# Modulation steps during the first layer's projections: from VectorE to GpSimd and ScalarE

## The chip, the cores and the metric

The kernel is one program on one core of a Trainium2 chip. The metric is the device time of one execution in microseconds (us); the median of three runs before the change is 1866.89 us. TensorE is called PE, VectorE DVE, ScalarE ACT, GpSimd POOL, and the queue that issues the DMAs SP.

## The reference

Two layers of a diffusion backbone, for 512 latent tokens and 256 context tokens of width 1024. The part that is changed is the modulation: two condition vectors, `c` for the latent tokens and `c_ctx` for the context tokens, each times a matrix of 1024 x 6144 per layer.

```python
def modulation(cond, w, b):
    m = jax.nn.silu(cond) @ w + b
    m = m.reshape(cond.shape[:-1] + (6, D_MODEL))
    return [m[..., i, None, :] for i in range(6)]

for l in range(DEPTH):
    mx = modulation(c, ada_w[l], ada_b[l])
    mc = modulation(c_ctx, ada_w[l], ada_b[l])
    hx = rmsnorm(x, norm_pre_mix[l]) * (1.0 + mx[1]) + mx[0]
    px = hx @ w_in[l]
    ...
    x = x + mx[2] * rmsnorm(yx, norm_post_mix[l])
    hx = rmsnorm(x, norm_pre_mlp[l]) * (1.0 + mx[4]) + mx[3]
    x = x + mx[5] * rmsnorm(sq_relu_mlp(hx, mlp_w1[l], mlp_w2[l]), norm_post_mlp[l])
```

Between these lines stand four token mixers (a gated delta net, a short convolution, a Hyena long convolution and a neighbourhood attention), fed by `px` and the same projection `pc` of the context.

## The kernel before

All large products are matmuls in three parts: `load_w` loads a weight tile of 128 x 512 (`raw`, three buffers), ACT casts it (`whi`, line 126), DVE subtracts to get the rest (`wlo`, line 127), and `mm3` (lines 138 to 140) makes three matmuls of each pair of halves. `big` (line 145 on) makes one output block of 128 columns with them: four `whi`/`wlo` pairs are held at a time, the result goes to `mx` (two PSUM buffers, latent tokens) and `mc` (one PSUM buffer, context tokens), and `dwconv` reads it out with a scaled copy on ACT (line 382) and two steps on DVE (lines 383 and 385).

The first two of the six modulation rows of layer 0 are made by matmuls at the start. The other ten row groups come from a generator, `mod_steps` (line 248). Each of its 80 steps loads a block of 128 x 1024 of the transposed matrix (`adrow`, two buffers, line 254) and makes, for each half of 512 and each condition, one multiplication with the broadcast condition `cbc` whose row sum goes to `part` (line 258). On DVE that is a SCALAR_TENSOR_TENSOR and the readout of its accumulator. A step of the stretch that matters has two halves and two conditions, so four such pairs. Every eighth step two small additions make the finished rows `mod`.

The steps are asked for at fixed places by `step_mods`: three after each of the four projections of keys and queries (`gdn_project`, line 561 on, `GPM = 3`), so 12 steps and 48 pairs, and the rest later, beside the mixers and the MLP. That is only the place in the program's text. A scheduler sets the order of each engine from the data that an instruction needs and its own costs; within one engine the order is then fixed. A step needs nothing but its block of weights, so the scheduler can place it early: in the trace the 12 steps run from 82 to 202 us, beside the projections and, more than half of them, beside the Hyena branch that comes ahead of these: `hyena_project` (three pairs of projections, with `spectrum` between them, whose sums and differences `ha` POOL makes at lines 472 and 473), and `hyena`, where ACT copies `odd` (line 510) out of PSUM before a long row of products on DVE. After that come the projections of keys and queries, `gdn_normalise` (DVE with two steps on POOL, lines 731 and 733), and the triangular solve of the delta net.

Of the kernel before, what the change touches and what calls it, by code (L numbers as in the profile page):

```python
# [9 lines left out]
F32 = mybir.dt.float32  # L10
F32R = mybir.dt.float32r
BF16 = mybir.dt.bfloat16
AF = mybir.ActivationFunctionType
# [32 lines left out]
class Net:  # L46
# [193 lines left out]
    def cond_rows(self, p):  # L240

        self.cbc = p.tile([128, 2, D], F32, tag="cbc", name="cbc")
        self.junk = p.tile([128, 512], BF16, tag="junk", name="junk")
        self.ring(p, "ad", 2)
        self.nc.sync.dma_start(self.cbc, self.cdr[0].partition_broadcast(128))

    def mod_steps(self):

        nc = self.nc
        for l, i in [(0, i) for i in range(2, 6)] + [(1, i) for i in range(6)]:  # L250
            conds = (0,) if l == 1 and i > 1 else (0, 1)
            for nb in range(i * 8, i * 8 + 8):
                raw = self.row_block()
                nc.sync.dma_start(raw, self.a["adaD"][32 + nb if l else nb - 16])
                for h in range(2):
                    hs = slice(h * 512, (h + 1) * 512)
                    for cnd in conds:
                        nc.vector.scalar_tensor_tensor(self.junk, raw[:, hs], 1.0, self.cbc[:, cnd, hs], op0=OP.mult,  # L258
                                                       op1=OP.mult, accum_out=self.part[:, l, cnd, nb, h:h + 1])
                if nb % 8 == 7:  # L260
                    s = slice(i * 8, i * 8 + 8)
                    for cnd in conds:
                        m = self.mod[:, l, cnd, s]
                        nc.vector.tensor_add(m, self.part[:, l, cnd, s, 0], self.part[:, l, cnd, s, 1])
                        nc.vector.tensor_add(m, m, self.adab[:, l, s])
                yield
# [1018 lines left out]
    def mix(self, l, hx):  # L1285
        nc, a = self.nc, self.a
        with_ctx = self.with_ctx = l == 0
        xs = [XSEG]
        segs = list(SEGS) if with_ctx else xs
        full = list(SEGS)  # L1290

        def scratch(nm, n):
            return [self.dp.tile([128, T], F32, name=f"{nm}{l}_{i}", tag=f"{nm}{l}_{i}") for i in range(n)]
        ydr, gdr = scratch("y", 2), scratch("g", 2)
        nad = {}
        for pr in range(2):
            for k in (("q", pr, 0), ("q", pr, 1), ("k", pr, 0), ("k", pr, 1), ("v", pr)):
                nm = "na" + "_".join(map(str, k)) + f"_{l}"
                nad[k] = self.dp.tile([128, T], F32, name=nm, tag=nm)
        w_in = a["win"][l]  # L1300
        fc_s = ExitStack()
        self.fcp = self.open(fc_s, "fc")
        with self.pool("tok") as self.tp:
            with self.pool("hyp") as hpp:
                if l:
                    self.fp_s = ExitStack()
                    fp = self.fp = self.open(self.fp_s, "flt", side="right")
                    hs = fp.tile([128, 512], F32, name="hs", tag="hs")
                    nc.sync.dma_start(hs[64:128], self.hsd)
                    self.sp_in = [(hs, self.spectrum_loads(1, 512, fp), 1, 512)]  # L1310
                u, x0 = self.hyena_project(l, w_in[8:14], hx, segs, hpp)
                self.spectra_at(l, 9)
                self.fp_s.close()
                with self.pool("hy") as hp:
                    self.hyena(l, u, x0, segs, ydr, hp)
            with self.pool("gdn") as gp:
                tok = {}
                rates = self.gdn_rates(l, a["wab"][l], hx, full, gp)
                tok["k"] = self.gdn_project(l, "k", 2, w_in, hx, full, self.psum)
                tok["q"] = self.gdn_project(l, "q", 0, w_in, hx, segs, self.psum)  # L1320
                if with_ctx:
                    self.cb_s.close()
                la, lbeta = self.gdn_normalise(tok, gp, rates)
                self.pg_s.close()
                self.po_s.close()
                with self.pool("psg", 4, space=PSUM) as self.pg, self.pool("pso", space=PSUM) as self.po:
                    na = self.na_project(w_in[14:20], hx, segs, full, nad)

                    def others(n):

                        for _ in range(n):
                            next(na)
                        self.gdn_values(l, tok, w_in, hx, full)
                    UX, qk = self.gdn_solve(l, tok, la, lbeta, gp, lambda: others(NA_STEPS))
                    self.gdn_run(tok, UX, qk, gp)
                    self.gdn_gate(l, w_in[0:8], hx, segs, gdr)
                    for _ in na:
                        pass
                    if with_ctx:
                        self.step_mods(MIX_STEPS)  # L1340
            ysp_s = ExitStack()
            yp = self.open(ysp_s, "ysp", side="right")
            e = segs[-1][0] + segs[-1][1]
            y = [[yp.tile([128, e], F32R, tag="ysp", name="ysp", bufs=16) for _ in range(2)] for _ in range(8)]
            with self.pool("na") as p, self.pool("nps", space=PSUM) as pn:
                for cb in range(2):
                    t = self.fc("yld")
                    nc.sync.dma_start(t[:, :e], ydr[cb][:, :e])
                    self.split(t[:, :e], y[4 + cb], slice(0, e))
                self.na_heads(l, nad, y[6:8], p, pn, with_ctx)  # L1350
                self.gdn_out(l, tok["q"], gdr, y[0:2], p, pn, segs)
                self.short_conv(l, w_in[20:26], hx, segs, y[2:4])
            if with_ctx:
                self.step_mods(24 - self.stepped)
        self.pm_s.close()
        fc_s.close()
        return y, ysp_s
# [188 lines left out]
    def run(self):  # L1546
        nc, a = self.nc, self.a
# [6 lines left out]
        cb = self.open(self.cb_s, "cb", side="right")  # L1554
# [3 lines left out]
        with self.pool("x0") as p:  # L1558
            self.cvec = p.tile([128, KB, 32], F32, tag="ccT", name="ccT")
            nc.sync.dma_start(self.cvec, a["ccT"])  # L1560
            nc.scalar.activation(self.cvec, self.cvec, AF.Silu)
            fl = self.filter_loads(fp)
            self.cdr = self.dp.tile([1, 2, D], F32, name="cdr", tag="cdr")
            flat = p.tile([128, 16], F32, tag="ccF", name="ccF")
            nc.sync.dma_start(flat, a["ccF"])
            nc.scalar.activation(flat, flat, AF.Silu)

            XS = p.tile([128, NBLK, D], F32, name="X0", tag="X0")
            self.first_scale(XS, p)
            nc.sync.dma_start(self.cdr[0].rearrange("c (p j) -> (c p) j", j=16), flat)  # L1570
            for i in (0, 2):
                self.mod_first_out(p, i, self.mod_first(p, i, True))
            self.first_turn(XS)
            top = self.filters(fl, fp)
            hx = self.new_act()
            self.ahead = [self.load_w(a["win"][0][10][:, 0:4], [4, 128])]
            for k0 in (0, 4):
                for c in range(2):
                    self.fac_pre(0, 0, c, k0, k0 + 4)
                if k0 == 0:  # L1580
                    ps = {i: self.mod_first(p, i, False, cb) for i in (1, 3)}
                    self.ahead += [self.load_w(a["win"][0][j][:, h:h + 4], [4, 128])
                                   for j, h in ((10, 4), (12, 0), (12, 4))]
                    self.setup2()
                self.first_norm(XS, p, hx, range(k0, k0 + 4))
                if k0 == 0:
                    for i in (1, 3):
                        self.mod_first_out(p, i, ps[i])
            nc.sync.dma_start(self.hsd, top[0][64:128])
            self.cond_rows(cb)  # L1590
            self.mods = self.mod_steps()
            ld = {L: self.spectrum_loads(0, L, fp) for L in DFT_LENS}
# [121 lines left out]
```

## Time and profile before

| what | value |
|---|---|
| runs | 1866.89, 1864.52, 1868.04 us; median 1866.89 |
| profiled execution | 1861.5 us, its span 1859.7 us |
| PE busy | 1772.7 us (95%) |
| DVE busy | 1267.8 us (68%) |
| ACT busy | 774.3 us (42%) |
| POOL busy | 263.1 us (14%), 273 instructions |

The profiled execution is 5.4 us shorter than the median of the runs; 1.8 us of it lie around its span. An engine runs its instructions in order, so one that waits holds up all that stand behind it on that engine. A row of the timeline gives start, duration, engine, line, what is written from what, the shape, a count where equal rows were put together, and in brackets the idle time before it and what ended it. Where the count is over one, the duration is that of all.

### The profile page before, as it was taken

What the parts mean: (1) busy time and instruction counts of PE and PEld (TensorE: products, weight loads), DVE (VectorE), ACT (ScalarE), POOL (GpSimd) and SP (SyncE); (2) the same over time, 40 slices, a digit from 0 to 9 for tenths busy, and PEclk for the clock granted to TensorE, in tenths of its full rate; (3) what the DMA queues carried; (4) which work ended last, traced back from release to release, by engine and by line L of the source; (5) the groups of instructions that cost most, each with busy time, mean ns of one, the idle gap of its engine ahead of it and who ended that gap; (6) DMA issues with size and microseconds to landing.
All of it is one profiled execution on the core that took longest, in us unless ns stands there. A gap on an engine that the chain in (4) does not pass through costs nothing. (4 is left out here: it accounts for less than half of the span.)

```text
span 1859.7 us, 29504 instructions
## 1 busy us (share of the span) xinstructions
PE 1772.7 (95%) x11170; PEld 1436.0 (77%) x11170; DVE 1267.8 (68%) x2366; ACT 774.3 (42%) x1548; POOL 263.1 (14%) x273
## 2 busy tenths in 40 slices
PE   6899888999999999999999999988899999999998
PEld 2667777788889888888888866777687787777776
DVE  5889898767776777655555586789756765544545
ACT  6333643466565222212222363463347662332323
POOL 0202531600120000000000041162330110000002
PEclk9999999999999999999999999999999999999999
DMA  8452213353565443433444233212235653322322
GB/s 300 150 182 97 91 63 114 118 147 124 182 212 170 146 129 117 123 124 114 130 125 131 83 141 111 69 60 91 73 103 152 210 182 98 106 98 78 115 80 85
DMA packets 105346, 233.55 MB, mean 126 GB/s; under 512 B 13202, under 2 KB 18132, under 8 KB 103925
## 3 DMA queue, kind: packets, MB, share of 16 engines
q1 hardware_dynamic: 105204, 231.68, 38.4%
q8 instruction: 88, 1.44, 0.3%
q14 instruction: 54, 0.43, 0.1%
HBM read 208.42 MB, written 23.21 MB: 125 GB/s over the span
## 5 line engine op out<-in xcount | busy, mean ns | idle before, releaser
L126 ACT CAST whi<-raw 128x512 fp32r<-128x512 f32 x444 | 273.6, 620 | 666.9 <-PE pb L140 269.8
L127 DVE TENSOR_TENSOR wlo<-raw,whi 128x512 fp32r<-128x512 f32 x444 | 317.1, 720 | 216.2 <-ACT whi L126 210.1
L140 PE MATMUL pb<-acth,wlo 128*128 128x512 f32 (+2 forms) x808 | 282.1, 349 | 0.2 <-DVE wlo L127 0.2
L139 PE MATMUL pb<-actl,whi 128*128 128x512 f32 (+2 forms) x808 | 281.8, 349 | 0.0
L138 PE MATMUL pb<-acth,whi 128*128 128x512 f32 (+2 forms) x808 | 280.9, 348 | 0.0
L138 PE MATMUL pb<-whi,hid 128*128 128x512 f32 x628 | 249.7, 398 | 0.8 <-ACT whi L126 0.6
L139 PE MATMUL pb<-wlo,hid 128*128 128x512 f32 x628 | 248.6, 396 | 0.3 <-DVE wlo L127 0.2
L140 PE MATMUL pb<-whi,hid 128*128 128x512 f32 x628 | 248.7, 396 | 0.0
L1498 DVE TENSOR_TENSOR acc<-acc,pb 128x1024 f32<-128x1024 f32 x96 | 117.2, 1221 | 152.6 <-PE pb L140 151.5
L258 DVE SCALAR_TENSOR_TENSOR junk<-adrow,cbc 128x512 bf16<-128x512 f32 x256 | 181.7, 710 | 6.0 <-DMA adrow<-in_adaD_dram 2.9
L139 PE MATMUL mx<-actl,whi 128*128 128x512 f32 x416 | 172.3, 414 | 1.4 <-POOL actl L374 1.2
L140 PE MATMUL mx<-acth,wlo 128*128 128x512 f32 x416 | 171.7, 413 | 0.5 <-DVE wlo L127 0.4
L138 PE MATMUL mx<-acth,whi 128*128 128x512 f32 x416 | 168.8, 406 | 2.1 <-ACT acth L235 1.2
L138 PEld LDWEIGHTS pb<-acth,whi 128*128 128x128 f32 x808 | 152.1, 188 | 20.4
L140 PEld LDWEIGHTS pb<-acth,wlo 128*128 128x128 f32 x808 | 152.0, 188 | 20.1 <-DVE wlo L127 0.4
L139 PEld LDWEIGHTS pb<-actl,whi 128*128 128x128 f32 x808 | 151.8, 188 | 20.1
L374 POOL TENSOR_TENSOR actl<-et,acth 128x256 fp32r<-128x256 f32 (+2 forms) x64 | 56.2, 896 | 732.7 <-DVE et L373 728.5
L138 PEld LDWEIGHTS pb<-whi,hid 128*128 128x128 f32 x628 | 117.8, 188 | 33.0 <-ACT hid L1399 5.4
L140 PEld LDWEIGHTS pb<-whi,hid 128*128 128x128 f32 x628 | 117.8, 188 | 29.5 <-DVE hid L1400 1.8
L139 PEld LDWEIGHTS pb<-wlo,hid 128*128 128x128 f32 x628 | 117.8, 188 | 28.3 <-DVE wlo L127 1.1
L138 PEld LDWEIGHTS mx<-acth,whi 128*128 128x128 f32 x416 | 79.5, 191 | 19.1 <-ACT acth L235 1.6
L139 PEld LDWEIGHTS mx<-actl,whi 128*128 128x128 f32 x416 | 79.7, 192 | 18.3 <-POOL actl L374 1.9
(398 smaller groups left out, 3015.3 us busy)
## 6 DMA issues: line engine op xcount, KB each, us to landing
raw<-in_w_dram SPq DMA_DIRECT2D x276, 256.0 KB, 2.8
adrow<-in_adaD_dram SPq DMA_DIRECT2D x80, 512.0 KB, 3.7
raw<-in_win_dram SPq DMA_DIRECT2D x104, 256.0 KB, 2.6
raw<-in_wout_dram SPq DMA_DIRECT2D x64, 256.0 KB, 3.0
X<-xdr SPq DMA_DIRECT2D x14, 512.0 KB, 4.4
X<-in_xin_dram SPq DMA_DIRECT2D x12, 512.0 KB, 5.1
xdr<-X SPq DMA_DIRECT2D x10, 512.0 KB, 2.8
adp<-in_adaP_dram SPq DMA_DIRECT2D x16, 256.0 KB, 5.5
```

Source lines behind the costliest of these rows:

```text
L126: self.nc.scalar.copy(hi, raw)
L127: self.nc.vector.tensor_sub(lo, raw, hi.bitcast(F32))
L138: mmul(o, st[0], mv[0], start=first, stop=False)
L139: mmul(o, st[0], mv[1], start=False, stop=False)
L140: mmul(o, st[1], mv[0], start=False, stop=last)
L258: nc.vector.scalar_tensor_tensor(self.junk, raw[:, hs], 1.0, self.cbc[:, cnd, hs], op0=OP.mult, op1=OP.mult, accum_out=self.part[:, l, cnd ...
L374: nc.gpsimd.tensor_sub(lo[:, r], t, hi[:, r].bitcast(F32))
L1498: op = nc.vector.tensor_add(o, o, ps)
```

## The change

While `mod_prod` is set (a pool, from the start until the projections of layer 0 are done), each pair on DVE becomes a multiplication on POOL and an activation with `Copy` on ACT, whose accumulator gives the row sum. The product of the first condition goes to a new tile `mp` with one buffer, that of the last condition overwrites the block `adrow` in place. The 68 steps that come later stay as they are.

```diff
--- before.py
+++ after.py
@@ cond_rows
         self.cbc = p.tile([128, 2, D], F32, tag="cbc", name="cbc")
-        self.junk = p.tile([128, 512], BF16, tag="junk", name="junk")
+        if not self.mod_prod:
+            self.junk = p.tile([128, 512], BF16, tag="junk", name="junk")
@@ mod_steps
                     for cnd in conds:
+                        if self.mod_prod:
+
+                            pr = raw[:, hs]
+                            if cnd != conds[-1]:
+                                pr = self.mod_prod.tile([128, 512], F32, tag="mp", name="mp")
+                            nc.gpsimd.tensor_mul(pr, raw[:, hs], self.cbc[:, cnd, hs])
+                            nc.scalar.activation(pr, pr, AF.Copy, accum_out=self.part[:, l, cnd, nb, h:h + 1])
+                            continue
                         nc.vector.scalar_tensor_tensor(self.junk, raw[:, hs], 1.0, self.cbc[:, cnd, hs], op0=OP.mult,
                                                        op1=OP.mult, accum_out=self.part[:, l, cnd, nb, h:h + 1])
@@ mix
                 if with_ctx:
+                    self.mod_prod = None
                     self.cb_s.close()
@@ run
+            self.mod_prod = cb
             self.cond_rows(cb)
```

The order of the instructions moves with it. On POOL, after the last of the eight `actl` of the first norm, the sums and differences `ha` of the first spectrum came next (line 472 is 481 after the change, 473 is 482). Before:

```order
L238 TENSOR_TENSOR actl<-et,acth 128x256 x8
L472 TENSOR_TENSOR ha<-hw 128x4x256
L473 TENSOR_TENSOR ha<-hw 128x4x256
L472 TENSOR_TENSOR ha<-hw 128x2x256
L473 TENSOR_TENSOR ha<-hw 128x2x256
L597 TENSOR_TENSOR A<-A,t_1137 128x512
```

Now five products (line 264) stand ahead of them, 23 more ahead of the second pair `ha`, and 20 more ahead of `A` of the Hyena branch:

```order
L238 TENSOR_TENSOR actl<-et,acth 128x256 x8
L264 TENSOR_TENSOR mp<-adrow,cbc 128x512
L264 TENSOR_TENSOR adrow<-adrow,cbc 128x512
L264 TENSOR_TENSOR mp<-adrow,cbc 128x512
L264 TENSOR_TENSOR adrow<-adrow,cbc 128x512
L264 TENSOR_TENSOR mp<-adrow,cbc 128x512
L481 TENSOR_TENSOR ha<-hw 128x4x256
L482 TENSOR_TENSOR ha<-hw 128x4x256
```

All 48 products stand one after the other on POOL, ahead of everything of the projections of keys and queries. On ACT, the place at the end of the second pair of Hyena projections and the start of `hyena` (`hyx` is the readout of a projection, `uT` the turned input, `odd` the copy that the Hyena products wait for). Before:

```order
L382 ACTIVATE hyx_1069<-mx,conv 128x512
L126 CAST whi<-raw 128x512
L382 ACTIVATE hyx_1069<-mc,conv 128x256
L577 COPY uT<-utps 128x256 x4
L510 COPY odd<-dps 128x256 x4
```

And now, with the sums of line 265 between them (382 is 391, 577 is 586, 510 is 519 after the change):

```order
L265 ACTIVATE mp,part<-mp 128x512
L391 ACTIVATE hyx_1068<-mx,conv 128x512
L265 ACTIVATE adrow,part<-adrow 128x512
L391 ACTIVATE hyx_1068<-mc,conv 128x256
L586 COPY uT<-utps 128x256 x2
L126 CAST whi<-raw 128x512
L586 COPY uT<-utps 128x256 x2
L265 ACTIVATE mp,part<-mp 128x512
L265 ACTIVATE adrow,part<-adrow 128x512
L519 COPY odd<-dps 128x256 x4
```

44 of the 48 sums stand ahead of the four copies `odd`; the first follows directly on the last of the four `ha` on ACT (line 467, now 476). The order on PE around these places is the same as before but for a few neighbours.

## Rows read from the trace of the kernel before

**Rows 1.** Windows view: window, length, busy us (instructions) by engine, granted clock, DMA.

```profile
60.00:82.00 22.00, 17.61 (x76) 11.66 (x76) 18.40 (x19) 7.07 (x13) 5.98 (x3) 0.91 0.34 124
82.00:150.00 68.00, 63.90 (x362) 48.95 (x361) 60.07 (x132) 20.16 (x41) 11.71 (x7) 0.98 0.41 142
...
160.00:205.00 45.00, 41.96 (x250) 36.08 (x249) 43.75 (x104) 22.86 (x41) 8.85 (x6) 0.99 0.35 118
205.00:330.00 125.00, 111.70 (x1300) 94.97 (x1300) 108.06 (x168) 55.72 (x128) 46.00 (x39) 0.93 0.26 89
```

**Rows 2.** Timeline of PE: three of its waits.

```profile
78.95 2.08 PE L508 MATMUL dps<-ha,dft 128*128 128x256 f32 x4 [3.04 <-POOL ha L472]
...
110.16 1.13 PE L521 MATMUL dps<-ha,dft 128*128 128x256 f32 x4 [2.90 <-POOL ha L472]
...
204.14 2.67 PE L763 MATMUL fTps<-cst,ktok 128*128 128x128 f32 x12 [2.65 <-DVE ktok L735]
```

**Rows 3.** Groups of DVE by line, 60-205 us, last row 60-150: busy, mean ns, idle.

```profile
L258 DVE SCALAR_TENSOR_TENSOR junk<-adrow,cbc 128x512 bf16<-128x512 f32 x48 | 36.1, 751 | 0.4
...
L258 DVE DVE_READ_ACCUMULATOR junk<-adrow,cbc 128x1 f32 x48 | 3.9, 82 | 0.0
...
L258 DVE SCALAR_TENSOR_TENSOR junk<-adrow,cbc 128x512 bf16<-128x512 f32 x26 | 18.7, 721 | 0.3
```

**Rows 4.** Timeline of DVE, 160 to 205 us.

```profile
170.23 0.68 DVE L127 TENSOR_TENSOR wlo<-raw,whi 128x512 fp32r<-128x512 f32 x1
...
194.82 0.68 DVE L258 SCALAR_TENSOR_TENSOR junk<-adrow,cbc 128x512 bf16<-128x512 f32 x1
...
197.10 1.36 DVE L258 SCALAR_TENSOR_TENSOR junk<-adrow,cbc 128x512 bf16<-128x512 f32 x1
...
199.62 2.34 DVE L258 SCALAR_TENSOR_TENSOR junk<-adrow,cbc 128x512 bf16<-128x512 f32 x1
...
203.40 0.68 DVE L735 TENSOR_TENSOR ktok<-rot 128x512 f32<-128x512 f32 x1
```

**Rows 5.** Line view of the final norm's squares on ACT: ns min/median/max, first and last start.

```profile
L332 ACT ACTIVATE junk<-acc x8: 629/636/637, 1839.4 to 1853.8; 128x512 f32<-128x512 f32 x8
L332 ACT ACTIVATION_READ_ACCUMULATOR junk<-acc x8: 185/186/188, 1840.0 to 1854.4; 128x1 f32 x8
```

**Rows 6.** Timeline of POOL at the end of the kernel: products of 128x512.

```profile
1841.35 1.29 POOL L333 TENSOR_TENSOR nt<-acc,frow 128x512 f32<-128x512 f32 x1 [0.58 <-DVE acc L1491]
1844.14 2.93 POOL L333 TENSOR_TENSOR nt<-acc,frow 128x512 f32<-128x512 f32 x2 [1.50 <-issue]
```

**Rows 7.** Timeline of ACT: the last two Abs, the first copy of the Hyena products.

```profile
71.10 1.15 ACT L467 ACTIVATE ha<-hw 128x512 f32<-128x512 f32 x2
...
128.90 0.37 ACT L510 COPY odd<-dps 128x256 f32<-128x256 f32 x1 [1.63 <-PE dps L508]
```

**Rows 8.** View of the tile adrow: its loads on SP, and their landing.

```profile
L254 SPq DMA_DIRECT2D adrow<-in_adaD_dram x80: 327/328/537, 59.3 to 1016.3; - x80
...
DMA to landing us min/median/max: 3.4/3.7/6.6
```

**Rows 9.** Timeline of POOL: the two pairs of sums and differences.

```profile
76.18 2.71 POOL L472 TENSOR_TENSOR ha<-hw 128x1024 f32<-128x1024 f32 x1 [15.67 <-DVE hn L469]
78.86 2.79 POOL L473 TENSOR_TENSOR ha<-hw 128x1024 f32<-128x1024 f32 x1
107.41 2.70 POOL L472 TENSOR_TENSOR ha<-hw 128x512 f32<-128x512 f32 x1 [25.77 <-PE mx L138]
110.07 1.72 POOL L473 TENSOR_TENSOR ha<-hw 128x512 f32<-128x512 f32 x1
```

**Rows 10.** Groups of POOL by line: sums of two broadcast operands.

```profile
L830 POOL TENSOR_TENSOR Dm<-cst,g 128x512 f32<-128x512 f32 x24 | 25.3, 1080 | 6.7 <-DVE UQ L849 3.6 <-ACT g L775 2.9
```

**Rows 11.** Timeline of DVE at the first pair of sums and differences.

```profile
76.01 6.18 DVE L127 TENSOR_TENSOR wlo<-raw,whi 128x512 fp32r<-128x512 f32 x3
```

**Rows 12.** Waits of ACT, 60 to 210 us: us in total, times, longest.

```profile
ACT whi L126 <- PE mc L139: 20.3, 15, 4.6
```

## The prediction

> **What bounds the kernel now.** Over the whole span PE is busy 95%, so the first question is whether the 48 pairs that leave DVE stand in PE's way at all. The windows view, cut at the ends of the stages, is read first. From 82 to 150 us, the stretch of the Hyena branch, DVE is busy 60.07 of 68 us, but PE 63.90 [rows 1]: both are nearly full, and the timeline of PE tells which waits for which. Its only long waits up to 150 us end with POOL, 3.04 us at 78.95 and 2.90 us at 110.16, both for `ha` [rows 2]; none ends with a step of the modulation or with something queued behind one. From 160 to 205 us DVE is fuller still, 43.75 of 45 us, and PE has 3.0 us idle [rows 1], of which 2.65 us end with the last step of the normalised keys, DVE's line 735 [rows 2]. From 205 to 330 us, in the triangular solve, PE idles 13.3 us [rows 1]. So up to 205 us PE has the work and DVE mostly only looks full; DVE stands in the way at 204 us and in the solve that starts there. Off the path: ACT, 20.16 of 68 us busy, and POOL, 11.71 [rows 1]. That is what the change draws on.
>
> **What it removes.** The 48 pairs took 36.1 + 3.9 = 40.0 us of DVE [rows 3]. 26 of them lie before 150 us [rows 3], where no wait of PE hangs on them: I count nothing for these. The other 22 lie beside the projections of keys and queries. What these give is read where they stand ahead of the keys: between the keys' scaling and line 735 there are three, 0.68, 1.36 and 2.34 us long [rows 4], with 0.08 us of readout each [rows 3]: 4.6 us. The keys then are ready 4.6 us earlier against PE's work, and the queries and the solve behind them too. Of this PE can use at most its idle time, 2.65 us at 204 and 13.3 us in the solve [rows 1, 2]; I take all of it: **-4.6 us**.
>
> **What it adds, on POOL and ACT.** A sum on ACT is priced by the only activation of this shape with a row sum: 0.636 us and 0.186 us for the accumulator, 0.82 us [rows 5]; 48 of them are 39.5 us. ACT has the room, from 82 to 150 us 47.8 us idle [rows 1]. But every sum waits for its product, and the casts and the readouts of PSUM are queued between the sums. What counts is therefore when POOL delivers.
>
> A product of 128 x 512 with two full operands took 1.29 us where it ran alone, and 1.46 us each where two ran beside DVE [rows 6]. The chain can be walked. The first sum stands on ACT behind the two Abs that end at 71.10 + 1.15 = 72.25 us [rows 7]. Products 1 and 2 have buffers of their own and are done by then: the first loads leave at 59.3 us and land within 6.6 us [rows 8], so by 69 us. Product 3 writes `mp` again and waits for the first sum: 72.25 + 0.82 = 73.1 us. From there POOL has no break: 42 more products up to number 44, and between them the two pairs `ha`, 5.5 and 4.4 us [rows 9]. The 44th sum ends at 73.1 + 9.9 + 0.8 + 42p = 83.8 + 42p, p being the price of a product, and the copy `odd` stands right behind it. Before, that copy came at 128.90 us [rows 7].
>
> - p = 1.08, the quickest POOL row of this shape, though of broadcast operands [rows 10]: 129.2 us, 0.3 us late.
> - p = 1.29: 138.0 us, 9.1 us late.
> - p = 1.46: 145.1 us, 16.2 us late.
>
> A product can also be held up by its block. A block's buffer comes free after the fourth sum, 0.82 us after the fourth product, and the next load lands 3.7 us later in the median [rows 8]; in that time POOL works through the other buffer, 4 x 1.29 = 5.2 us. 4.5 against 5.2 us is enough for the median, not for the slowest landing of 6.6 us. I take the middle of the two rows of the same operation, p = 1.38: 141.8 us, 12.9 us late.
>
> Does PE notice? The readouts of `mx` and `mc` on ACT stand between the same sums, `mc` has one buffer, and the order of PE is unchanged; it waits for each readout, then for `uT`, then for the Hyena products. The lead that the casts have does not help there. So I count the delay in full: **+12.9 us**. A DVE that is freed earlier doesn't shorten it, since the Hyena products wait for `odd`. `ha` of the first pair comes behind product 5, at 73.1 + 3 x 1.38 = 77.2 us instead of 76.18, and the second pair behind product 28 about 7 us late: PE's two waits for it grow, but this is the same delay and not counted again. The 12 loads stay 12; on SP the weight loads that stand behind a block's load now wait for a sum on ACT, which is again the same delay. `A` on POOL comes after all 48 products, in time. The new tile costs no time.
>
> **The sum.** 12.9 - 4.6 = +8.3 us on the profiled execution's 1861.5 us, 1869.8 us. That execution lies 5.4 us under the median of the runs, so for the median 1866.9 + 8.3 = **1875 us**. About 0.2%, 3.7 us, is what can be told from no change.
>
> **The rivals.**
>
> *The products keep pace, and it gets faster.* If p is at the quick end, 1.08 us, the delay is 0.3 us and the relief of 4.6 us remains: -4.3 us, 1862.6 us. It is faster by more than 0.2% only if the delay stays under 0.9 us, that is p under 1.10. For it: 24 rows of this shape at 1.08 us [rows 10]. Against: these read two broadcast operands, and no row with two full operands is under 1.29 us. A gain that I do not see on DVE, since 26 pairs leave a full engine before 150 us, is in its chance too. 0.20.
>
> *DVE and POOL get in each other's way, and it gets clearly slower.* Beside the first pair `ha`, three subtractions `wlo` took 6.18 us [rows 11], 2.06 us each where one alone takes 0.68 [rows 4]; the second `ha` of half that size took as long, 2.70 us beside 2.71 [rows 9]. In the changed order 17 DVE instructions with two SBUF operands stand from the first sum to `odd` (12 `wlo`, 4 of the spectrum, one product). If each holds a product up for its own 0.69 us, that is 11.7 us over 42 products, p = 1.38 + 0.28 = 1.66, and the delay 24.6 us: +20 us, 1887 us. Against it as the likeliest: the pairs that leave DVE had two SBUF operands too, and 17 instructions are 11.7 of 69 us. 0.25. [...]
>
> *The delay is hidden, and nothing can be measured.* For it: ACT's casts wait for PE to release a weight buffer 15 times, 20.3 us in all [rows 12], so weights are ahead of need. If the leads swallow 5 to 12 us of the delay, the sum is within 3.7 us of zero: 1867 us. Against it: the single `mc` buffer. 0.17.
>
> *The change doesn't do what it says*: by the order it does, though the 12 steps run beside the Hyena branch, not beside the projections of keys and queries.
>
> **How the numbers follow.** The forecast, +4 to +16 us (p from 1.28 to 1.56), has 0.38. With the second rival's 0.25, slower has 0.63; the same 0.17; faster 0.20. [...] Four more such waits are +4 us: 1891.
>
> **What would show it.** Right: POOL busy about 66 us more, with few gaps from 73 us until about 145 us; products of 1.3 to 1.5 us; ACT's idle time there ended by the products of line 264; the first `odd` of `hyena` at about 142 us; the keys' last step at about 204 + 8 us. Wrong: products near 1.1 us or `odd` near 129 us (then the relief decides), or `odd` late with PE no later at 150 us (a lead that I did not count), or products over 1.6 us with `wlo` over 1 us (the second rival). If the keys' last step shows no 4.6 us against `odd`, that term falls.

## The result and the profile after

The changed kernel takes 1884.14 us, median of four runs (1882.12 to 1886.43), against 1865.70 us for the kernel before, also of four runs: a ratio of 1.0109, 95% interval 1.0091 to 1.0127. It is slower, by 18.4 us in the medians; the forecast was 8 us slower. The profiled execution took 1882.1 us with a span of 1880.3, so 20.6 us more on either.

The windows view of the changed kernel, in the columns of [rows 1]:

```profile
60.00:82.00 22.00, 17.81 (x81) 12.46 (x82) 18.32 (x22) 9.98 (x22) 11.39 (x8) 0.96 0.42 152
82.00:150.00 68.00, 53.21 (x242) 39.09 (x241) 39.35 (x60) 41.95 (x112) 58.67 (x43) 0.89 0.47 161
...
160.00:205.00 45.00, 40.41 (x232) 34.91 (x232) 35.20 (x67) 18.10 (x33) 8.38 (x6) 0.92 0.22 70
205.00:330.00 125.00, 109.88 (x845) 93.56 (x843) 106.15 (x161) 60.12 (x134) 41.40 (x32) 0.95 0.21 69
```

From 82 to 150 us DVE's work went from 60.07 to 39.35 us, as it should, POOL's from 11.71 to 58.67, ACT's from 20.16 to 41.95. But PE, which had no long wait on DVE there, went from 63.90 to 53.21, and its granted clock from 0.98 to 0.89. The groups of POOL from 60 to 170 us (busy, mean ns, idle before):

```profile
L264 POOL TENSOR_TENSOR mp<-adrow,cbc 128x512 f32<-128x512 f32 x24 | 34.3, 1430 | 18.4 <-DMA adrow<-in_adaD_dram 12.7 <-ACT mp L265 5.7
L264 POOL TENSOR_TENSOR adrow<-adrow,cbc 128x512 f32<-128x512 f32 x24 | 33.4, 1393 | 1.8
```

A product takes 1.41 us in the mean, between the two rows of [rows 6]. The timeline of POOL shows the chain from the third product on, its two breaks for a block that had not landed, the second pair `ha`, and the 44th product:

```profile
74.05 1.30 POOL L264 TENSOR_TENSOR mp<-adrow,cbc 128x512 f32<-128x512 f32 x1 [4.88 <-ACT mp L265]
...
107.23 1.69 POOL L264 TENSOR_TENSOR mp<-adrow,cbc 128x512 f32<-128x512 f32 x1 [1.44 <-DMA adrow<-in_adaD_dram]
...
119.20 1.27 POOL L481 TENSOR_TENSOR ha<-hw 128x512 f32<-128x512 f32 x1
...
139.47 1.29 POOL L264 TENSOR_TENSOR mp<-adrow,cbc 128x512 f32<-128x512 f32 x1 [1.34 <-DMA adrow<-in_adaD_dram]
...
143.44 1.28 POOL L264 TENSOR_TENSOR adrow<-adrow,cbc 128x512 f32<-128x512 f32 x1
```

On ACT, the 44th sum and the first `odd` of `hyena`, which came at 128.90 us before [rows 7]:

```profile
145.44 0.63 ACT L265 ACTIVATE adrow<-adrow 128x512 f32<-128x512 f32 x1
145.97 0.20 ACT L265 ACTIVATION_READ_ACCUMULATOR adrow<-adrow 128x1 f32 x1
147.43 0.37 ACT L519 COPY odd<-dps 128x256 f32<-128x256 f32 x1 [1.27 <-PE dps L517]
```

The view of ACT's waits from 72 to 147 us (total, times, longest) has 21.3 us for products; before, ACT waited there for PE alone in its three longest groups:

```profile
ACT adrow L265 <- POOL adrow L264: 10.7, 15, 1.9
ACT mp L265 <- POOL mp L264: 10.6, 16, 1.3
```

PE's waits, to be read beside [rows 2]: the first wait for `ha` is 0.45 us longer, the second 6.72 instead of 2.90 us (and the four matmuls behind it take 2.07 us, not 1.13). The wait for the keys, 2.65 us before, is nearly gone, and one of 4.22 us for the queries has come, which was not there before:

```profile
80.76 2.08 PE L517 MATMUL dps<-ha,dft 128*128 128x256 f32 x4 [3.49 <-POOL ha L481]
...
120.53 2.07 PE L530 MATMUL dps<-ha,dft 128*128 128x256 f32 x4 [6.72 <-POOL ha L481]
...
169.56 7.10 PE L630 MATMUL yps<-dfi,q 128*128 128x128 f32 x32 [3.50 <-DVE q L621]
...
220.99 1.53 PE L772 MATMUL fTps<-cst,ktok 128*128 128x128 f32 x12 [0.37 <-DVE ktok L743]
...
233.32 2.22 PE L772 MATMUL fTps<-cst,qtok 128*128 128x128 f32 x12 [4.22 <-DVE qtok L744]
```

Followed from place to place, the lag is:

| place (start, us) | before | after | late by |
|---|---|---|---|
| second pair `ha` | 107.41 | 119.20 | 11.8 |
| first `odd` of `hyena` | 128.90 | 147.43 | 18.5 |
| first inverse products `yps` | 148.90 | 169.56 | 20.7 |
| last step of the keys on DVE | 203.40 | 220.26 | 16.9 |
| last step of the queries on DVE | 211.01 | 232.50 | 21.5 |
| span | 1859.7 | 1880.3 | 20.6 |

So the delay up to `odd` is larger than forecast, two more microseconds are lost right behind it, and the lead that the keys win back is gone at the queries.

### The profile page after: what moved, and what is told of

It reads as the page before. It is cut to its first block, busy times and chain, and to the rows that moved or that the text cites. A ratio compares the mean times of both kernels' runs of the same rounds, so it can differ in the third digit from the quotient of the medians.

```text
span 1880.3 us, 29553 instructions
## 1 busy us (share of the span) xinstructions
PE 1779.1 (95%) x11170; PEld 1440.2 (77%) x11170; DVE 1251.0 (67%) x2270; ACT 806.3 (43%) x1644; POOL 327.0 (17%) x321
## 3 DMA queue, kind: packets, MB, share of 16 engines
q8 instruction: 88, 1.44, 0.3%
## 5 line engine op out<-in xcount | busy, mean ns | idle before, releaser
L127 DVE TENSOR_TENSOR wlo<-raw,whi 128x512 fp32r<-128x512 f32 x444 | 320.9, 728 | 236.8 <-ACT whi L126 231.3
L267 DVE SCALAR_TENSOR_TENSOR junk<-adrow,cbc 128x512 bf16<-128x512 f32 x208 | 145.3, 698 | 4.1 <-DMA adrow<-in_adaD_dram 1.5
L138 PE MATMUL mc<-acth,whi 128*128 128x256 f32 x272 | 81.2, 299 | 15.4 <-DVE cv L394 10.0
```

Source lines behind the costliest of these rows:

```text
L127: self.nc.vector.tensor_sub(lo, raw, hi.bitcast(F32))
L138: mmul(o, st[0], mv[0], start=first, stop=False)
```

## The experiments

All are compared with runs of the kernel before on the same chip. The three short_ runs, relief_nal, the two no_sums runs and free_queues leave work out and serve for the times alone. "Late" is against the places in the table above; a minus is early.

| run | ratio (95% interval) | `odd` late | keys late | queries late |
|---|---|---|---|---|
| the change | 1.0109 (1.0091, 1.0127) | 18.5 | 16.9 | 21.5 |
| short_sums | 1.0143 (1.0126, 1.0159) | 25.4 | 20.1 | 24.7 |
| short_products | 1.0016 (1.0006, 1.0026) | 3.9 | -1.6 | 3.0 |
| short_pairs | 1.0009 (0.9997, 1.0021) | 0.2 | -3.6 | 1.0 |
| relief_nal | 0.9999 (0.9988, 1.0011) | 0.8 | -4.3 | -3.6 |
| no_sums | 1.0116 (1.0097, 1.0136) | 19.1 | 14.0 | 18.6 |
| ha_on_dve | 1.0063 (1.0045, 1.0081) | 14.2 | 9.7 | 14.3 |
| no_sums_ha_dve | 1.0048 (1.0032, 1.0063) | 13.1 | 8.3 | 12.9 |
| ha_dve_before | 0.9977 (0.9964, 0.9991) | -7.1 | 0.6 | 0.6 |
| free_queues | 1.0052 (1.0036, 1.0067) | 14.4 | 9.0 | 13.7 |
| ha_dve_own_queue | 1.0093 (1.0078, 1.0109) | 24.0 | 18.6 | 23.2 |
| one_condition | 1.0071 (1.0058, 1.0085) | 10.1 | 7.4 | 12.1 |
| split_six | 1.0141 (1.0124, 1.0157) | 10.1 | 22.1 | 26.7 |
| late_six | 1.0122 (1.0108, 1.0136) | 3.4 | 15.4 | 20.1 |
| last_two_ha | 1.0019 (1.0006, 1.0032) | -7.6 | 4.7 | 8.2 |
| last_four_ha | 1.0021 (1.0009, 1.0033) | -6.5 | 10.2 | 10.3 |
| later_steps | 1.0153 (1.0137, 1.0169) | 3.5 | -0.6 | 4.0 |
| later_steps_ha | 1.0058 (1.0038, 1.0078) | -7.6 | -13.0 | -8.4 |

### Product or sum

short_sums:

```diff
-nc.scalar.activation(pr, pr, AF.Copy, accum_out=...)
+nc.scalar.activation(pr[:, 0:16], pr[:, 0:16], AF.Copy, accum_out=...)
```

> Leaves out most of each sum: the 48 activations add up 16 columns of the product instead of 512; the 48 products on POOL stay whole. Theory A (the chain of products on POOL sets the delay, and ACT, which runs in order, hands it on to the copies that stand behind the sums): the first odd of the Hyena products still at 140 us or later, time +12 to +20 us over the kernel before. Rival B (the 39 us of sums on ACT keep casts and readouts waiting): ACT is 20 us or more less busy from 82 to 150 us, odd within 4 us of 128.9, time within 5 us of the kernel before.

short_products (both products in place, `ws` 16 columns; the sums over the whole half as before):

```diff
-nc.gpsimd.tensor_mul(pr, raw[:, hs], self.cbc[:, cnd, hs])
+nc.gpsimd.tensor_mul(raw[:, ws], raw[:, ws], self.cbc[:, cnd, ws])
```

> Leaves out most of each product: 16 columns on POOL, in place, for both conditions; the 48 sums on ACT stay whole, 512 columns. Theory A: POOL has no chain left, the first odd at 128.9 us within 3 us, time between -5 and +3 us against the kernel before. Rival B: ACT's sums are all there, odd 10 us late or more, time +12 to +20 us.

With short sums ACT is busy 24.06 us from 82 to 150 us instead of 41.95, and the time grows: `odd` starts at 154.31 us, and ACT only waits longer (72 to 147 us):

```profile
ACT adrow L265 <- POOL adrow L264: 23.1, 20, 3.4
ACT mp L265 <- POOL mp L264: 17.4, 18, 1.5
```

With short products ACT has all its 39 us of sums, and `odd` is 3.9 us late and the time 3 us over. ACT's occupancy is not the cause; the products on POOL are. That short_sums is worse than the change itself goes with the order: 35 products stand there ahead of the second pair `ha`, not 28, and it begins at 126.14 us, 6.9 us later than in the change; `odd` too is 6.9 us later.

### By which way the products delay PE

The sums left out, the four `ha` on POOL as they are (no_sums):

```diff
-nc.scalar.activation(pr, pr, AF.Copy, accum_out=...)
```

> The changed kernel without the 48 sums (left out; the accumulators are set to zero once at the start): the 48 products are all on POOL, the four ha too, and ACT has nothing to wait for. In this order the second pair ha stands behind 36 products, 30 of them after the first pair. Theory A2 (the delay has two ways: ACT's queue behind the sums, and POOL's own queue in front of ha): the second pair begins at 118 to 124 us instead of 107.41, the first odd at 140 to 150 us, time +10 to +20 us. If ACT's queue were the only way: odd within 4 us of 128.9, time within 4 us of the kernel before.

The change with `ha` on DVE (ha_on_dve), and both edits together (no_sums_ha_dve):

```diff
-nc.gpsimd.tensor_add(hp[:, :, 0, :], ...)
-nc.gpsimd.tensor_sub(hp[:, :, 1, :], ...)
+nc.vector.tensor_add(hp[:, :, 0, :], ...)
+nc.vector.tensor_sub(hp[:, :, 1, :], ...)
```

> The changed kernel with the four sums and differences ha on DVE instead of POOL, so no ha stands behind a product any more. Theory A (ACT's queue inherits the whole chain of products): the chain is shorter by the 8.1 us that the four ha took on POOL and by nothing else, the first odd at about 139 us, time +9 to +13 us over the kernel before. Rival D (the second pair ha on POOL behind 28 products is the harm; it began 11.8 us late, and PE waited 6.7 us for it): odd within 4 us of 128.9, time within 4 us of the kernel before.

> As no_sums, sums left out, and the four ha on DVE: the same 48 products on POOL beside the same DVE work, but no engine waits for a product any more. Theory A2: nothing is late, odd at 128.9 us within 4 us, time within 4 us of the kernel before. Rival C (the products themselves are the harm, since DVE and POOL block each other): time +8 us or more.

> The kernel before with the four ha on DVE and nothing else: the control of ha_on_dve and no_sums_ha_dve. PE's waits for ha (3.04, 0.68 and 2.90 us) shrink by the difference between 2.7 us on POOL and about 1.3 us on DVE: -1 to -4 us if the path to odd carries it to the end, 0 if it is given back at a later wait.

Without any sum the time is as bad as with all of them. The way is then mainly POOL's own queue, in which 36 products stand ahead of the second pair `ha`, 28 in the change; PE's timeline in no_sums:

```profile
127.30 1.22 PE L530 MATMUL dps<-ha,dft 128*128 128x256 f32 x2 [14.62 <-POOL ha L481]
```

With `ha` off POOL and the sums kept, the loss is 11.7 us (0.63%), as theory A had it from a chain shorter by 8.1 us, with `odd` at 143.13 instead of 139 us. But with both taken away, where no compute engine should wait for a product, `odd` is still 13.1 us late, only 1.1 us less than with the sums, and the intervals of the two ratios overlap. So theory A's time came out, but it is not shown that its way, ACT's sums, made it. ACT's and SP's waits in no_sums_ha_dve (72 to 150 and 60 to 150 us):

```profile
ACT whi L127 <- DMA raw<-in_win_dram: 19.1, 5, 8.0
...
SPq L256 <- POOL adrow L265: 40.8, 8, 5.5
```

ACT waits for weights, and the weights stand on SP behind the loads of blocks whose buffers POOL has not freed. Against the kernel before with the same `ha` on DVE, which is 0.23% faster than it, the products alone cost 0.7%. So the next pair took that queue away as well: the blocks are loaded from POOL's own queue (free_queues from no_sums_ha_dve, ha_dve_own_queue from ha_on_dve).

```diff
-nc.sync.dma_start(raw, self.a["adaD"][...])
+nc.gpsimd.dma_start(raw, self.a["adaD"][...])
```

> As no_sums_ha_dve (48 products on POOL, sums left out, ha on DVE), and the blocks adrow are loaded by POOL's own DMA queue instead of SP's. Theory A3 (what is late there is a third queue: SP issues the weight loads in order behind loads of blocks that wait for POOL's products; ACT waited 19.1 us for weights): those waits go, the first odd at 129 us or earlier, time within 4 us of the kernel before. Rival C (DVE and POOL block each other): odd stays at 138 us or later, time +6 us or more.

> The whole change (products on POOL, sums on ACT, nothing left out) with the ha on DVE and the blocks loaded by POOL's own DMA queue: of the three queues that stand behind the products only ACT's is left. Theory A3 with ACT as a way of its own: odd at 136 to 142 us, time +7 to +13 us. If SP's queue was what was left: odd within 4 us of 128.9, time within 4 us of the kernel before.

Theory A3 did not hold: SP no longer waits for POOL, of ACT's waits for weights one of 5.9 us is left, and `odd` is 14.4 us late all the same. What is left is rival C, and the timeline of DVE in free_queues shows it:

```profile
82.89 3.69 DVE L481 TENSOR_TENSOR ha<-hw 128x1024 f32<-128x1024 f32 x1
...
90.38 0.41 DVE L521 TENSOR_TENSOR eo<-dps,odd 128x256 f32<-128x256 f32 x1
...
96.66 3.14 DVE L539 TENSOR_TENSOR hw<-eo 128x512 f32<-128x512 f32 x1
...
109.36 3.44 DVE L128 TENSOR_TENSOR wlo<-raw,whi 128x512 fp32r<-128x512 f32 x1 [2.41 <-ACT whi L127]
```

Beside the first of these rows, POOL:

```profile
82.97 1.29 POOL L265 TENSOR_TENSOR adrow<-adrow,cbc 128x512 f32<-128x512 f32 x1
84.21 1.28 POOL L265 TENSOR_TENSOR mp<-adrow,cbc 128x512 f32<-128x512 f32 x1
85.57 2.14 POOL L265 TENSOR_TENSOR adrow<-adrow,cbc 128x512 f32<-128x512 f32 x1
```

The same `ha` took 1.22 us in ha_dve_before, where POOL has no products, and a `wlo` 0.68 us [rows 4]. The groups of `wlo` from 74 us to the first `odd`, in ha_dve_before (to 122 us) and in free_queues (to 144 us):

```profile
L127 DVE TENSOR_TENSOR wlo<-raw,whi 128x512 fp32r<-128x512 f32 x11 | 7.5, 679 | 0.3 <-ACT whi L126 0.3
L128 DVE TENSOR_TENSOR wlo<-raw,whi 128x512 fp32r<-128x512 f32 x12 | 18.0, 1504 | 4.8 <-ACT whi L127 4.8
```

It reaches PE: in these stretches PE's waits of over 1 us are none in ha_dve_before, and in free_queues four that all end with DVE, for `eo` (3.3 us), `wlo` (3.2), `ha` (2.2) and `hw` (1.1). DVE is busy 54.11 us from 82 to 150 us with 67 instructions, against 40.16 us with 62 in no_sums_ha_dve, where the products are the longer (1.51 us in the mean, here 1.43). The `eo` beside the products, which have one operand in PSUM, took 0.41 or 0.42 us each, in ha_dve_before 0.42 or 0.43. The 3.69 us are about the 1.22 us of the `ha` and the two products that ran beside it one after the other (1.29 and 1.28 us), and the third product took 2.14 us, 0.86 more than the second.

ha_dve_own_queue, where ACT's sums wait as well, is worse than ha_on_dve. The products ran beside DVE in every run that kept them whole, so none of these runs shows ACT's way, or SP's, by itself. What was not tried is each way with the others switched off and the order of all engines held; the order is made anew for each kernel, so the amounts of single ways are not to be added.

### Dose and place

one_condition, the second condition alone on POOL and ACT:

```diff
-if self.mod_prod:
+if self.mod_prod and cnd == conds[-1]:
```

> Only the second condition goes to POOL and ACT (24 products, in place), the first stays on DVE (24 pairs). Theory A: 24 products of 1.4 us are done well before the copy odd is needed, odd at 128.9 us within 4 us, time within 4 us of the kernel before. Rival C (each product on POOL costs the other engines its own share, by the way DVE and POOL block each other): half of the loss, +8 to +10 us.

split_six and late_six hold the products of steps 7 to 12 behind the first `A` of the Hyena branch; (`self.held` is that addition on POOL); in late_six steps 1 to 6 stay on DVE:

```diff
+with self.tc.issue_after(self.held):
     nc.gpsimd.tensor_mul(pr, raw[:, hs], self.cbc[:, cnd, hs])
```

> The changed kernel, but the products of steps 7 to 12 are held on POOL behind the first A of the Hyena branch; steps 1 to 6 stay where they are. Nothing is left out. Theory A: 24 products and the four ha from 74 us on are over at 74 + 22 x 1.42 + 8.1 = 113 us, the first odd at 129 to 133 us; the other 24 fill POOL from 143 to about 180 us and delay the second, short Hyena part; time +2 to +8 us over the kernel before. Rival E (moving the pairs to POOL and ACT costs time wherever they stand): +16 to +20 us, as with all 48 early.

> Steps 1 to 6 on DVE as in the kernel before, steps 7 to 12 on POOL and ACT, held behind the first A of the Hyena branch. Nothing is left out. Theory A: odd at 128.9 us within 2 us; the keys' last step earlier than 203.4 us or up to 3 us later, by how much ACT's sums delay the second, short Hyena part; time 0 to +6 us. If the relief of DVE were worth what was predicted: -4 us.

All three missed, and in one manner: I had counted only whether the chain is over before `odd` is needed. In one_condition a sum stands in front of a copy `odd` on ACT, its product stands behind `ha` on POOL, and ACT's timeline has

```profile
118.97 0.63 ACT L265 ACTIVATE adrow<-adrow 128x512 f32<-128x512 f32 x1 [7.09 <-POOL adrow L264]
119.51 0.18 ACT L265 ACTIVATION_READ_ACCUMULATOR adrow<-adrow 128x1 f32 x1
119.60 0.35 ACT L533 COPY odd<-dps 128x256 f32<-128x256 f32 x1
```

In late_six `odd` is 3.4 us late, but 24 sums stand among the readouts and casts of the keys' projections:

```profile
150.83 0.63 ACT L268 ACTIVATE mp<-mp 128x512 f32<-128x512 f32 x1 [4.61 <-POOL mp L267]
...
183.04 0.63 ACT L268 ACTIVATE mp<-mp 128x512 f32<-128x512 f32 x1 [5.15 <-POOL mp L267]
```

As these traces read, the harm lies less in the total of the chain than in each sum or product that stands in front of something that PE needs soon; in late_six two products also stand ahead of a `q` on POOL for which PE waits 3.47 us. That moving such a piece takes the harm away was not tried. A small dose, with `ha` on DVE and only the last steps on POOL (10 for last_two_ha, 8 for last_four_ha, counted from 0):

```diff
-if self.mod_prod:
+if self.mod_prod and step >= 10:
```

> A small dose: the ha on DVE, steps 1 to 10 on DVE as in the kernel before, only steps 11 and 12 (8 products) on POOL and ACT; nothing is left out. The 8 products have POOL to themselves, and the first of their sums stands behind the last copy but one of the queries on ACT. If the finding holds (a chain on POOL costs where a queue stands behind it, and here hardly one does): odd at about 122 us, the keys 3 us or more earlier than 203.4 us, time -2 to -6 us. If even 8 products delay what stands behind them: 0 to +6 us.

> As last_two_ha with steps 9 to 12 (16 products) on POOL and ACT; nothing is left out. Eight more sums stand among ACT's readouts of the queries' projections: each can hold these up by a product of 1.3 to 1.5 us. Time -3 to +6 us; if the harm grows with the number of sums ahead of readouts, later than last_two_ha by 4 us or more.

Even 8 products lose against the kernel before (0.19%, interval 0.06 to 0.32%; some 0.4% against ha_dve_before, which has the same `ha` on DVE), and the 7.6 us by which `odd` is early are gone at the keys. With 16 products the keys are 5.5 us later still and the time the same within its interval.

### What the relief is worth

short_pairs leaves the pairs on DVE and makes them short; relief_nal also moves two subtractions `nal` that follow the normalisation:

```diff
-nc.vector.scalar_tensor_tensor(self.junk, raw[:, hs], 1.0, self.cbc[:, cnd, hs], ...)
+nc.vector.scalar_tensor_tensor(self.junk[:, 0:16], raw[:, ws], 1.0, self.cbc[:, cnd, ws], ...)
```

```diff
-nc.gpsimd.tensor_sub(lo[:, :e], t[:, :e], hi[:, :e].bitcast(F32))
+with self.tc.issue_after(self.q_last):
+    nc.vector.tensor_sub(lo[:, :e], t[:, :e], hi[:, :e].bitcast(F32))
```

> The 48 pairs stay on DVE as in the kernel before, but of 16 columns each (most of the products left out): POOL and ACT have nothing to do for them, DVE is relieved of about 30 us. It prices the relief alone. As predicted: -4.6 us. Rival: a part of the three pairs ahead of the keys was DVE waiting for POOL (2.34 and 1.36 us against 0.68 alone), which falls on the next DVE instruction instead: -3 to 0 us.

> The kernel with the short pairs (16 columns, products left out) and one edit: the first two subtractions nal go from POOL to DVE and are held there behind the queries' last step. In short_pairs the keys came 4.2 us earlier but the queries 1.0 us later, and three small DVE steps between them took 1.84, 0.88 and 1.80 us where 0.21 to 0.25 is usual, each beside a nal on POOL. Theory F (the relief was used up by DVE waiting for POOL): these take 0.25 us or less, the queries come 3 us or more earlier than in short_pairs, time -2 to -4 us against the kernel before. Rival G (the solve waits for something else): queries earlier, time within 1.5 us of the kernel before.

In short_pairs the keys are 3.6 us early and the queries 1.0 us late. DVE's timeline between the two, with the two `nal` of POOL's timeline below:

```profile
201.59 1.84 DVE L696 TENSOR_SCALAR w<-e 128x96 f32<-128x96 f32 x1
...
208.77 0.88 DVE L703 SCALAR_TENSOR_TENSOR w<-abt,w 128x96 f32<-128x96 f32 x1
...
210.18 1.80 DVE L704 SCALAR_TENSOR_TENSOR la<-w,ea 128x48 f32<-128x48 f32 x1
```

```profile
201.20 2.17 POOL L1144 TENSOR_TENSOR nal<-na,nah 128x768 fp32r<-128x768 f32 x1
...
209.62 2.29 POOL L1144 TENSOR_TENSOR nal<-na,nah 128x768 fp32r<-128x768 f32 x1
```

The changed kernel has the same three rows, at 222.09, 229.28 and 230.68 us (1.84, 0.87 and 1.80 us). The first and the last ran beside a `nal`; the middle one ended as the second `nal` began and ran beside POOL's cast `nah` ahead of it (208.61 us, 0.94 us), not beside a `nal` as I had expected. The first, a TENSOR_SCALAR, reads one SBUF operand and no second, and took 1.84 us all the same. In the kernel before these three took 0.20, 0.25 and 0.21 us, and the first `nal` had met a pair instead (the one of 2.34 us in [rows 4]), which cost the keys and not the queries. With `nal` moved, the three take 0.20, 0.26 and 0.21 us and the queries are 3.6 us early, and still the time is that of the kernel before, as rival G had it. The lead is there until the solve, where PE waits for something that the profile does not show (L970 before, L976 in relief_nal, L979 in the change):

```profile
PE zp L970 <- issue: 1.1, 1, 1.1
```

```profile
PE zp L976 <- issue: 4.4, 1, 4.4
```

```profile
PE zp L979 <- issue: 4.6, 1, 4.6
```

In the profiled executions the kernel before is the exception: the change waits 4.6 us there, and eleven other versions 3.3 (ha_dve_before) to 5.5 us (short_products). So the times of short_pairs (3.9 us there) and relief_nal hold some 3 us more of this wait than the kernel before, and what sets it is open. The last attempt has the relief without POOL and ACT:

```diff
-GPM = 3
+GPM = 1
```

> The kernel before with 4 instead of 12 steps beside the projections of keys and queries (GPM = 1), the other 8 on DVE at the later places; nothing is left out. Relief without POOL and ACT: as in short_pairs the keys about 4 us earlier; if the lead is given back at later waits, time within 2 us of the kernel before, if not -2 to -5 us.

> As later_steps, and the four ha on DVE. In ha_dve_before odd came 7 us earlier, but DVE, full with the pairs of the last steps, had the keys ready at the same time as before. If DVE in that stage is what takes the lead back: keys 5 us or more earlier, time -5 to -10 us. If the solve's own waits take it back: -2 to -4 us, as ha_dve_before.

Both lose, since the eight steps cost more where they then stand: from 500 to 1000 us PE is busy 483.94 us in later_steps and 498.49 before, and its longest waits there are 8.9 us for ACT and 4.8 us for DVE, before 1.5 us. Their early part tells something, though: with `ha` on DVE and the late pairs gone, the keys are 13.0 us early, with the pairs there (ha_dve_before) not at all. So in that stage the pairs do hold DVE back once the work ahead of it comes early. Of all versions only ha_dve_before beats the kernel before, by 0.23% (0.09 to 0.36%); its profile, of one of its slowest executions (1863.74 us of 1857.40 to 1864.13), has no lead left at the queries, so where that gain arises is open.

## Why the prediction was wrong

The direction held, and the products on POOL are the cause: short_products, with all sums on ACT, lost 0.16%, short_sums 1.43%. The way was only in part as I had it: I let ACT's sums hand the delay on, and the delay is as large without a single sum (no_sums). The size did not hold. Forecast 8.3 us on the profiled execution, measured 20.6; by the forecast's own terms the difference is:

| term | forecast | measured | difference |
|---|---|---|---|
| delay of the first `odd` | 12.9 | 18.5 | 5.6 |
| from `odd` to `yps` | 0 | 2.2 | 2.2 |
| relief, up to the queries and the end | -4.6 | 0 | 4.6 |
| sum | 8.3 | 20.7 | 12.4 |

That the sum meets the span's 20.6 us is partly luck: PE's unseen wait in the solve added 3.5 us on the way, and that was made up in the later stages. In other runs the lag at the queries is not the loss at the end: 14.3 us late in ha_on_dve, and its span is 9.1 us longer.

**The delay of `odd`.** The price of a product, p = 1.38, was nearly right: from 74.05 to 144.72 us there are 70.67 us, less 8.13 for the four `ha` and 2.78 for the two breaks, which is 59.8 us for 42 products, 1.42 each. Of the 5.6 us, 1.8 come from that, -1.8 from `ha` (8.13, not 9.9 us), 0.95 from the start of the third product. The rest are steps that I had set to zero. "From there POOL has no break" failed: the two breaks cost 1.44 + 1.34 = 2.78 us. It was not the slow landing that I had thought of, for the block behind the second break landed in 4.5 us and the product behind the first began 4.8 us after its block's load. On SP both loads left late, 0.42 us behind a weight load:

```profile
102.05 0.33 SPq L118 DMA_DIRECT2D raw<-in_wab_dram  x1
102.47 0.38 SPq L255 DMA_DIRECT2D adrow<-in_adaD_dram  x1
...
134.42 0.33 SPq L118 DMA_DIRECT2D raw<-in_win_dram  x1
134.84 0.38 SPq L255 DMA_DIRECT2D adrow<-in_adaD_dram  x1
```

The fourth sums had freed the buffers at 101.0 and 133.4 us, 1.5 us earlier each, but the weight load stood ahead and waited for a `wlo` on DVE, which ended at 102.02 and 134.39 us. I had let weight loads wait behind those of blocks, not blocks behind weights. And "the copy `odd` stands right behind it" is not so, for the 44th sum ended 1.45 us behind its product, 0.65 more than the 0.8 us of [rows 5], and `odd` waited 1.27 us more for PE, whose own chain of `uT` and `dps` had been held by the sums ahead.

**From `odd` to `yps`.** "`A` on POOL comes after all 48 products, in time" was right and not the point. Products 47 and 48, at 153.18 (1.83 us) and 155.09 us (1.62 us), ran beside the four spectrum steps on DVE: the two of line 538 took 2.37 us together, and those of line 539 as well, where each pair took 1.28 us before. That is what the second rival had, at one place, on the path: 2.2 us. These products were that late because of a third break of 5.05 us ahead of product 45, whose block's load left SP at 145.67 us, again behind weight loads.

**The relief.** The step that failed is "I take all of it". On the keys it was there: their lag is 3.8 us smaller than that of `yps`. But behind it stood the queries, on the same DVE, held by POOL's `nah` and `nal`; and part of the 4.6 us was never the pairs' own time: two of the three took 1.36 us beside POOL's step of line 733 and 2.34 us beside `nal`, against 0.68 alone, and with the pairs short three other DVE steps were longer there (1.84, 0.88 and 1.80 us). short_pairs prices the relief at +0.09% (-0.03 to 0.21%): nothing, with the longer wait in the solve in it.

**The rivals.** The products did not keep pace (1.41, not 1.08 us). The second rival came nearest in time, 1887 us, but not by its condition: it needed p = 1.66. In the mean the products of the change were about 0.13 us longer than the 1.28 us of one that ran beside no DVE step with two SBUF operands (142.08 us), 6.3 us in 48. The third, a hidden delay, fell: PE lost 10.7 us of work from 82 to 150 us. The range went from 1862 us, for p = 1.08, to 1891: the second rival's 1887 and 4 us for four more waits of PE, each with four matmuls behind it that take 2.08 and not 1.13 us [rows 2]. No run shows those 4 us: in the change the granted clock from 82 to 150 us was 0.89, 0.98 before, and one such group, behind the second wait for `ha`, took 2.07 us instead of 1.13.

**What I had not seen** is that the delay has several ways, and that taking one or two of them away leaves most of it. I had written of `ha` and of SP's loads that they are "the same delay and not counted again". As a sum that was right. As an explanation it was too narrow: with the sums away `odd` is 19.1 us late, with `ha` away 14.2, with both away 13.1, and with the blocks off SP's queue as well 14.4, where DVE's held instructions are what the trace shows. What each way has in the change itself stays open.

## What to carry to other kernels

Before work is moved to an idle engine, compare the duration of one piece there with the distance between the pieces in the new order: to have `odd` on time, a product could have taken (128.9 - 83.8) / 42 = 1.07 us, and it took 1.42. Here the idle engine was no free room, since its own work for PE stood behind the moved pieces (the second pair `ha` began 11.8 us late), its results were awaited inside the queue of an engine that feeds PE (ACT waited 21.3 us for products from 72 to 147 us), and its pieces ran beside the instructions of another (in free_queues an `ha` on DVE took 3.69 us, not 1.22). One late piece at the head of a queue was enough: in one_condition a sum waited 7.09 us for its product, and `odd` behind it, whose four matmuls began at 116.09 us and took 2.08, came at 119.60. The total occupancy of ACT, 42 of 68 us, did not tell it. And the relief counted only as far as the next wait, the 4.22 us for the queries: read who is next behind it on the same engine before it is put in the sum.

## What the runs showed of the hardware

- In free_queues a DVE instruction with two SBUF operands took about its own time and that of two POOL products: 3.69 us for an `ha` that took 1.22 us in ha_dve_before, beside products of 1.29 and 1.28 us. The `eo`, with one operand in PSUM, took 0.41 or 0.42 us beside the products.
- That added time stayed when the longer instruction was made short: in the kernel before a pair took 2.34 us beside a `nal` of 2.18 us, against 0.68 alone, and in short_pairs three small steps of 0.20 to 0.25 us took 1.84, 0.88 and 1.80 us beside two `nal` and a cast. The first of these has one SBUF operand. In relief_nal, with the `nal` on DVE, they took 0.20, 0.26 and 0.21 us.
- Before the same matmuls of the solve PE waited 1.1 us in the kernel before, 4.6 us in the change and 3.3 to 5.5 us in eleven other versions, for nothing that the profile shows. What sets it is open.
